# Weight preparation of a decoder layer in six steps: casts placed behind the sums and the evictions, sample rows transposed later

## The chip, the core and the metric

The kernel runs on one core of one Trainium2 chip. The metric is the device time of one execution in microseconds (us). The engines are named as in the profile: PE is TensorE (matmul; PEld its weight loads), DVE is VectorE, ACT is ScalarE, POOL is GpSimd, SP is SyncE, which here only issues transfers. Each engine works through its own queue in order.

## The reference, cut to what matters

One layer of a decoder trunk, for a prompt of 1024 tokens and 8 × 4 sample tokens, 1056 columns in all, width 1024, hidden width 2816:

```python
def trunk_layer(x, ...):
    h = layer_norm(ALPHA * x + 0.5 * swiglu(x, f1_w1, f1_w3, f1_w2), ln1_g, ln1_b)
    z = h @ w_in + b_in                      # 42 blocks of 128 columns: q, k, v, gMLP, gates
    ...                                      # dilated attention (3 groups), gMLP branch
    mix = (sigmoid(ga) * (att @ w_oa) + sigmoid(gb) * (yb @ w_ob)) @ w_out
    h = layer_norm(ALPHA * h + mix, ln2_g, ln2_b)
    h = layer_norm(ALPHA * h + 0.5 * swiglu(h, f2_w1, f2_w3, f2_w2), ln3_g, ln3_b)
def swiglu(x, w1, w3, w2):
    return (silu(x @ w1) * (x @ w3)) @ w2
```

The outputs are `h`, the last keys and values of each attention group, and the normalised rows of the open gMLP chunk.

## The kernel before, in words

**Arithmetic.** Everything is fp32. A product is made of three fp32r matmuls: each operand is split into a high half (a cast on ACT, line 253) and a low half (a subtraction on DVE, line 254), and high·high, high·low and low·high are added up in PSUM (`mm3`, line 242). Columns are worked in four chunks of 264.

**Seven products.** Most weight blocks go through a Strassen scheme of the Winograd form: two blocks times two chunk pairs take seven products instead of eight, in the order 1, 2, 6, 7, 5, 4, 3. This is done in `hidden` (the hidden blocks of both feed-forwards), `seven` (their down-projections) and `pair` (13 pairs of blocks of the input projection, `f` = 0 to 12). After each product its PSUM banks are evicted, partly on ACT (in `pair` line 1034), partly on DVE (line 1043), and `between` runs. There are three `mm` banks and five `ax` banks.

**Weight preparation.** `prep` makes the weights of the next block in the time of the present one. It is a Python generator: each `next` traces one step. It loads the raw weights `ab` (line 376) and `cd` (line 377) into a pool of two buffers, forms the sums `s12` (lines 386 and 387) and `s34` (392 and 394) on POOL, or on DVE where the block has 768 columns instead of 1024 (the down-projections) and for the first blocks, and splits `ab`, `s12`, the last part of `cd` (called `dd`) and `s34` into high and low halves. Products 1 and 2 use `ab`, 6 and 5 use `s12`, 7 and 3 use `s34`, 4 uses `dd`. The first step is traced when the present block begins, the next ones by `between` after its products 1, 2, 6 and 7.

**Order.** A planner orders the instructions of each engine: it goes by the order of tracing and by priorities, and by when it estimates an instruction to be ready. Loads and evictions have raised priority (`high_priority`, `urgent`). `fenced` adds an ordering: what is traced inside it comes, on DVE, ACT and SP (not on POOL), behind the last eviction traced so far. The background queues (`tick`, `step`) are fenced; the steps of `prep` are not.

**Sample rows.** In the pair stage, after each of the nine pairs that hold queries, keys and values, `sample_rows` transposes the 32 sample columns of the two blocks on PE (line 1375), copies them out on DVE (1377) and stores them from SP (1381, 1386). It is a background generator that is resumed three times after each product and pauses first.

Of the kernel before, what the change touches and what calls it, by code (L numbers as in the profile page):

```python
# [16 lines left out]
ALU = mybir.AluOpType  # L17
# [4 lines left out]
P = 128  # L22
D = 1024
# [36 lines left out]
REST = 3  # L60
GAP = 4
AFTER = 100
LATE = 16
MID = 3
HOP = (4, 1, 4)
# [18 lines left out]
class Trunk:  # L84
# [285 lines left out]
    def prep(self, src, f, H, engine):  # L370

        nc = self.nc
        lo, hi, n = slice(0, H), slice(H, 2 * H), 2 * H
        with self.tc.high_priority(offset=URGENT):
            ab, cd = self.R([P, D])[:, :n], self.R([P, D])[:, :n]
            nc.sync.dma_start(ab, src[1])
            dma = nc.sync.dma_start(cd, src[0])
        self.copy_state(dma, 2)
        tt = engine.tensor_tensor
        ah, al = self.W([P, D]), self.W([P, D])  # L380
        self.split(ah[:, :n], al[:, :n], ab)
        if f == LASTW2:
            h34, l34 = self.held([P, D], F32R), self.held([P, D], F32R)
        yield
        s12 = self.Q([P, D])
        tt(s12[:, lo], cd[:, lo], cd[:, hi], op=ALU.add)  # L386
        tt(s12[:, hi], s12[:, lo], ab[:, lo], op=ALU.subtract)  # L387
        yield
        s34 = self.Q([P, D])
        h12, l12 = self.W([P, D]), self.W([P, D])  # L390
        self.split(h12[:, :n], l12[:, :n], s12[:, :n])
        tt(s34[:, lo], ab[:, lo], cd[:, lo], op=ALU.subtract)  # L392
        yield
        tt(s34[:, hi], ab[:, hi], s12[:, hi], op=ALU.subtract)  # L394
        part = lambda h, l, o=0: [((h, l), o + k * P) for k in range(H // P)]
        if n == D:
            dd = self.S([P, D], F32R)
            self.split(dd[:, lo], dd[:, hi], cd[:, hi])
            p4 = part(dd[:, lo], dd[:, hi])
        else:  # L400
            p4 = []
            for h, l, w in ((ah, al, D - n), (h12, l12, H - (D - n))):
                o = H + len(p4) * P
                self.split(h[:, n : n + w], l[:, n : n + w], cd[:, o : o + w])
                p4 += part(h, l, n)[: w // P]
        yield
        if f != LASTW2:
            h34, l34 = self.S([P, D], F32R), self.S([P, D], F32R)
        self.split(h34[:, :n], l34[:, :n], s34[:, :n])
        self.L[f] = {  # L410
            1: part(ah, al), 2: part(ah, al, H), 5: part(h12, l12), 6: part(h12, l12, H),
            7: part(h34, l34), 3: part(h34, l34, H), 4: p4,
        }
        yield

    def product(self, t, p, f, first):
        while any(p not in t for t in self.T):
# [257 lines left out]
    def ffn(self, w13, w2p, w2, i, mode, resid):  # L675
        nc, preps = self.nc, {}
        plain = PLAIN[: 1 if i == 0 else 2]
        blocks = [f for f in range(FB) if f not in plain] + [FB + g for g in range(NG * (KB // 2))]
        after = dict(zip(blocks, blocks[1:]))

        def begin(f):
            if f < FB:
                preps[f] = self.prep(w13[f], f, KH * P, nc.gpsimd if f > 2 else nc.vector)
            else:
                preps[f] = self.prep(w2p[f - FB], f, HP, nc.vector)
            next(preps[f])

        if i == 0:
            self.lns = {}
            self.T, self.L = ({}, {}), {}  # L690
            units = self.lead_in(w13)
            self.new_x(1)
            self.consts()
            s0, s1 = (self.spread(j, self.Y, self.A, self.nc.vector) for j in range(2))
            begin(1)
            with self.tc.high_priority(offset=URGENT):
                for k in range(2):
                    self.load_x(self.nc.sync, 3, k, 0, KH)
            for c, work in enumerate((((2,), s0, s0, 1), ((3,), s0, 1, 1), (s1, s1, s1, 1), (1, s0))):
                self.hidden8(units, 0, c)  # L700
                for x in work:
                    if isinstance(x, tuple):
                        self.new_x(*x)
                    else:
                        next(preps[x] if x == 1 else x, None)
            self.bg.extend((s0, s1))
        else:
            lead, s1 = self.early
            lns, self.lns = self.lns, {}
            self.drain(lns[NC - 2])  # L710
            self.step(self.bg, 1)
            begin(1)
            for c in range(NC):
                self.drain(lns.pop(c))
                if c == NC - 1:
                    self.bg.append(s1)
                    self.step(self.bg, 2)
                for f, u in zip(plain, lead):
                    self.hidden8(u, f, c)
                    if c:  # L720
                        with self.chained():
                            next(preps[1], None)
            lead = self.early = None
        self.sqs = {}
        self.Y = self.A = None
        loads = deque(self.load_sums(resid))
        total = len(loads)

        def ready(f):
            for _ in preps.pop(f):  # L730
                pass
            if f in after:
                begin(after[f])

        def between(f, bg, slow=0):
            if after.get(f) in preps:
                next(preps[after[f]], None)
            self.tick(bg, slow)

        def load(n):  # L740

            with self.tc.high_priority(offset=URGENT):
                while loads and total - len(loads) < n:
                    loads.popleft()()

        for f in blocks[: FB - len(plain)]:
            ready(f)
            if f == FB - 1:
                load(2)
            count = iter(range(1, 8))  # L750

            def step():
                between(f, STEPS["strassen"])
                if f == FB - 1:
                    load(min(HEAD, 2 + 4 * next(count)))

            self.hidden(f, step)
            del self.L[f]
        self.T = ({}, {})
        self.normed = [None] * NC  # L760
        self.out(w2, i, mode, ready, between, load)

    def load_hidden(self, f):
# [61 lines left out]
    def out(self, w2, i, mode, ready, between, load):  # L825
# [101 lines left out]
        for c in range(NC):  # L927
            early = 6 if c == 0 else 0
            if mode != "out":
                self.hold_normed(c)  # L930
                if c == 2:
                    self.early = [self.unit(self.a["wzp"][n], slot=True, ahead=AFTER) for n in range(CHUNKED)]
            for n in range(KB):
# [14 lines left out]
    def tables(self):  # L948
# [8 lines left out]
        for g in range(3):  # L957
            nc.sync.dma_start(oh[g], a["ohP"][:, g])
        yield from self.pause(LATE)
        for g in range(3):  # L960
# [16 lines left out]
        nc.sync.dma_start(rs, a["relS"])  # L977
        yield from self.pause(LATE)
        for i, pair in enumerate(PAIRS):
# [107 lines left out]
    def widen(self):  # L1087
# [13 lines left out]
        preps = {}  # L1101
# [15 lines left out]
        for n in range(CHUNKED, NLEAD):  # L1117
            w = self.unit(a["wzp"][n])
            if n == NLEAD - 1:
                begin(0)  # L1120
            for c in (1, 3, 0, 2):
                self.gate8(w, DENSE[n], c, AF.Sigmoid, STEPS["lead"], 1)
                if n == NLEAD - 1:
                    next(preps[0], None)
        self.A = None
        for f in range(NZ):
            for _ in preps.pop(f):
                pass
            if f < NZ - 1:
                begin(f + 1)  # L1130

            def between():
                if f + 1 in preps:
                    next(preps[f + 1], None)
                self.tick(STEPS["strassen"], 1)

            self.pair(f, between)
            del self.L[f]
# [230 lines left out]

    def sample_rows(self, *blocks):  # L1370
        nc, a = self.nc, self.a
        yield from self.pause(4)
        p = self.ax_tile()[:NS, : 2 * P].rearrange("p (s x) -> p s x", s=2)
        for x, (_, t) in enumerate(blocks):
            nc.tensor.transpose(p[:, x], t[:, NP:], self.ident)
        st = self.M([NS, 2, P])
        nc.vector.tensor_copy(st, p)
        for x, (nb, _) in enumerate(blocks):
            s, g, hp = nb // 6, (nb % 6) // 2, nb % 2
            L = GROUPS[g][0]  # L1380
            nc.sync.dma_start(
                self.sD[g, s, 2 * hp : 2 * hp + 2].rearrange("h t e -> t h e"),
                st[:, x].rearrange("t (h e) -> t h e", h=2),
            )
            if s:
                nc.sync.dma_start(a[f"ws{g}"][:, L - 4 :, 256 * (s - 1) + P * hp : 256 * (s - 1) + P * hp + P], st[:, x])
# [522 lines left out]
```

## Time and profile before

| | |
|---|---|
| time, median of 3 runs | 2154.41 us (2153.32 to 2157.72) |
| time of the profiled execution | 2154.51 us |
| its span | 2152.5 us |
| PE busy | 2122.6 us, 99% |
| DVE, ACT, POOL busy | 1549.5, 889.4, 317.1 us |

The span runs from the first to the last instruction of the program; the time of the execution lies 2.0 us above it. By stretch: from 50 to 475 us the hidden blocks of the first feed-forward run, to 670 its down-projection, from about 790 to 1060 the pairs of the input projection, to 1490 attention, gMLP and output projections, to 1920 and 2085 the second feed-forward. A line of the timeline gives start, duration, engine, line, operation, tiles (output<-inputs) and count; brackets give the idle time of the engine before it and what ended it. W, S, R, Q and M are the tile pools: W and S hold split weights, R raw weights, Q sums.

### The profile page before, as it was taken

To read this page: it belongs to the slowest core of one execution; us is meant where nothing else is said; L and a number is where in the kernel's file an instruction comes from. 1 tells how busy PE (TensorE), PEld (TensorE's weight loads), DVE (VectorE), ACT (ScalarE), POOL (GpSimd) and SP (SyncE) were. 2 spreads that over 40 slices of the span, in tenths; PEclk is the share of its full clock that TensorE was granted. 3 is DMA by queue.
4 is the path that set the end of the run, shared out by engine and by line. 5 is a ranking of instruction groups with operands and counts; after the bars stand their busy time and mean duration, and the time that the engine had idled before them with its cause. 6 is when DMAs were issued, how large, how long until landed. Compare 5 with 4: busy or idle time off the path is not lost.

```text
span 2152.5 us, 43254 instructions
## 1 busy us (share of the span) xinstructions
PE 2122.6 (99%) x17307; PEld 2085.6 (97%) x17307; DVE 1549.5 (72%) x2727; ACT 889.4 (41%) x1680; POOL 317.1 (15%) x249
## 2 busy tenths in 40 slices
PE   9999999999999999999999999999999999999997
PEld 8999999999999999999988889999999999999997
DVE  8877767747789834777767758787667777657887
ACT  5444444422124634333476544164444444421224
POOL 0432322200000011323000000000323323100000
PEclk9999999999999999999999999999999999999998
DMA  4444555598885335676865765423454554596852
GB/s 155 145 140 170 183 166 168 189 338 315 327 325 176 130 103 177 201 231 198 296 211 187 223 190 177 154 110 110 144 174 156 183 173 153 194 408 267 311 186 81
DMA packets 168377, 426.51 MB, mean 198 GB/s; under 512 B 24352, under 2 KB 59792, under 8 KB 165488
## 3 DMA queue, kind: packets, MB, share of 16 engines
q1 hardware_dynamic: 167744, 423.21, 56.4%
q8 instruction: 135, 2.21, 0.4%
q10 hardware_dynamic: 432, 0.54, 0.1%
q14 instruction: 66, 0.54, 0.1%
HBM read 304.31 MB, written 165.57 MB: 218 GB/s over the span
## 4 chain that ended last, share of the span: by engine, by line
PE 89%; DVE 4%; DMA 4%; POOL 1%; issue 1%; ACT 0%; SPq 0%; ACTq 0%; DVEq 0%; POOLq 0%
PE ax L242 46%; PE mm L242 39%; DMA R<-wz 1%; PE ax L1206 1%; DMA M<-kv 1%; DMA S<-cD 1%; PE ax L1255 1%; PE ax L1232 1%; DVE W L254 1%; DMA S<-hD 0%; DVE S L632 0%; POOL Q L392 0%; POOL Q L387 0%; DVE S L254 0%; PE ax L621 0%
## 5 line engine op out<-in xcount | busy, mean ns | idle before, releaser
L242 PE MATMUL mm<-S,W 128*128 128x264 f32 x5400 | 713.6, 287 | 8.0 <-ACT S L253 2.3
L242 PE MATMUL ax<-S,W 128*128 128x264 f32 x5400 | 708.6, 285 | 1.3 <-ACT S L1034 1.1
L242 PEld LDWEIGHTS mm<-S,W 128*128 128x128 f32 x5400 | 677.1, 189 | 21.0 <-issue 7.0
L242 PEld LDWEIGHTS ax<-S,W 128*128 128x128 f32 x5400 | 678.5, 189 | 4.0 <-ACT S L1034 2.4
L242 PE MATMUL ax<-S,S 128*128 128x264 f32 x3240 | 475.9, 284 | 1.0 <-ACT S L1034 0.5
L242 PEld LDWEIGHTS ax<-S,S 128*128 128x128 f32 x3240 | 427.7, 188 | 1.7 <-DVE S L1043 0.9
L242 PE MATMUL mm<-S,S 128*128 128x264 f32 x2280 | 359.4, 286 | 2.6 <-DVE S L925 2.6
L242 PEld LDWEIGHTS mm<-S,S 128*128 128x128 f32 x2280 | 311.0, 189 | 3.9 <-issue 2.9
L253 ACT CAST W<-R 128x256 fp32r<-128x256 f32 (+2 forms) x175 | 130.6, 764 | 307.5 <-PE mm L242 139.9
L386 POOL TENSOR_TENSOR Q<-R 128x512 f32<-128x512 f32 x49 | 68.1, 1390 | 800.8 <-DMA R<-w13a 198.2
L254 DVE TENSOR_TENSOR W<-R,W 128x256 fp32r<-128x256 f32 (+2 forms) x175 | 154.6, 887 | 23.3 <-ACT W L253 21.7
L253 ACT CAST W<-Q 128x1024 fp32r<-128x1024 f32 (+1 forms) x78 | 76.8, 984 | 217.2 <-POOL Q L387 88.1
L820 DVE SCALAR_TENSOR_TENSOR S<-ax,S 128x264 f32<-128x264 f32 x240 | 99.7, 429 | 66.1 <-PE ax L242 65.7
L462 DVE TENSOR_TENSOR S<-ax,M 128x264 f32<-128x264 f32 x82 | 32.6, 433 | 144.7 <-PE ax L242 144.7
L254 DVE TENSOR_TENSOR S<-Q,S 128x1024 fp32r<-128x1024 f32 (+1 forms) x78 | 113.6, 1456 | 5.5 <-ACT S L253 5.4
L110 POOL CAST S<-ones 128x1 fp32r<-128x1 f32 x36 | 12.5, 355 | 675.7 <-PE ax L242 226.0
L254 DVE TENSOR_TENSOR W<-Q,W 128x1024 fp32r<-128x1024 f32 (+1 forms) x78 | 90.6, 1161 | 29.6 <-ACT W L253 29.6
L253 ACT CAST S<-Q 128x1024 fp32r<-128x1024 f32 (+1 forms) x78 | 76.7, 984 | 68.4 <-PE ax L242 49.8
L254 DVE TENSOR_TENSOR S<-S,M 128x528 fp32r<-128x528 f32 x72 | 84.6, 1175 | 2.5 <-ACT M L253 0.7
L253 ACT CAST S<-R 128x512 fp32r<-128x512 f32 (+1 forms) x62 | 42.0, 677 | 98.9 <-DMA sumsA<-S 40.6
L387 POOL TENSOR_TENSOR Q<-Q,R 128x512 f32<-128x512 f32 x49 | 81.0, 1653 | 2.7
L394 POOL TENSOR_TENSOR Q<-R,Q 128x512 f32<-128x512 f32 x49 | 79.7, 1627 | 1.2
(209 smaller groups left out, 2042.5 us busy)
## 6 DMA issues: line engine op xcount, KB each, us to landing
ws<-st SPq DMA_DIRECT2D x144, 256.0 KB
S<-sumsA SPq DMA_DIRECT2D x63, 528.0 KB
S<-sumsB SPq DMA_DIRECT2D x63, 528.0 KB
M<-kv SPq DMA_DIRECT2D x96, 256.0 KB
sumsA<-M SPq DMA_DIRECT2D x90, 264.0 KB
sumsB<-M SPq DMA_DIRECT2D x90, 264.0 KB
R<-w13b SPq DMA_DIRECT2D x44, 512.0 KB
R<-w13a SPq DMA_DIRECT2D x42, 512.0 KB
```

Source lines behind the costliest of these rows:

```text
L110: self.nc.gpsimd.tensor_copy(t[:, 0, :1] if len(shape) == 3 else t[:, :1], self.ones[:, :1])
L242: mm = lambda a, b, s, e: nc.tensor.matmul(o, a[:, cc], b, start=s, stop=e, skip_group_check=True)
L253: a = self.nc.scalar.copy(hi, src)
L254: b = self.nc.vector.tensor_tensor(lo, src, hi.bitcast(F32), op=ALU.subtract)
L386: tt(s12[:, lo], cd[:, lo], cd[:, hi], op=ALU.add)
L387: tt(s12[:, hi], s12[:, lo], ab[:, lo], op=ALU.subtract)
L394: tt(s34[:, hi], ab[:, hi], s12[:, hi], op=ALU.subtract)
L462: go(one, 5, False, lambda x: tt(h[:, x, 1], one[x], p7[:, x], op=ALU.add))
L820: nc.vector.scalar_tensor_tensor(y(x, r, e), bank[x], HALF, y(x, r, e), op0=ALU.mult, op1=ALU.add)
L1206: m = nc.tensor.matmul(pS[h][:, r, :nk], q[e, i * P : (i + 1) * P], k[e, k0 : k0 + nk], start=True, stop=True)
L1232: nc.tensor.transpose(pT[r][:, h, o], s[:, r, h, o], self.ident)
L1255: nc.tensor.matmul(pv[0][e, (i % 4) * P : (i % 4 + 1) * P], V[:, i - (nb - 1) + b, e], sT[:, r, h, b * P : b * P + P], start=b == 0, stop= ...
```

## The change

Four things change. In `prep` the split of `ab` moves from the first step to the second, behind the sums of `s12`; the split of `s12` moves from the third step to the fourth, and the third step holds only the first sum of `s34`. All steps but the first are traced inside `fenced`, through a new function `advance`, in both the feed-forwards and the pairs. The preparation of the very first pair is resumed once more before its pair begins. `sample_rows` pauses for 8 resumptions instead of 4.

```diff
+ROWS = 8
...
             dma = nc.sync.dma_start(cd, src[0])
         self.copy_state(dma, 2)
         tt = engine.tensor_tensor
-        ah, al = self.W([P, D]), self.W([P, D])
-        self.split(ah[:, :n], al[:, :n], ab)
         if f == LASTW2:
             h34, l34 = self.held([P, D], F32R), self.held([P, D], F32R)
         yield
         s12 = self.Q([P, D])
         tt(s12[:, lo], cd[:, lo], cd[:, hi], op=ALU.add)
         tt(s12[:, hi], s12[:, lo], ab[:, lo], op=ALU.subtract)
+        ah, al = self.W([P, D]), self.W([P, D])
+        self.split(ah[:, :n], al[:, :n], ab)
         yield
         s34 = self.Q([P, D])
+        tt(s34[:, lo], ab[:, lo], cd[:, lo], op=ALU.subtract)
+        yield
         h12, l12 = self.W([P, D]), self.W([P, D])
         self.split(h12[:, :n], l12[:, :n], s12[:, :n])
-        tt(s34[:, lo], ab[:, lo], cd[:, lo], op=ALU.subtract)
-        yield
         tt(s34[:, hi], ab[:, hi], s12[:, hi], op=ALU.subtract)
...
+    def advance(self, gen):
+        if gen is not None:
+            with self.fenced():
+                next(gen, None)
...
         def between(f, bg, slow=0):
-            if after.get(f) in preps:
-                next(preps[after[f]], None)
+            self.advance(preps.get(after.get(f)))
             self.tick(bg, slow)
...
                 if n == NLEAD - 1:
-                    next(preps[0], None)
+                    for _ in range(2 if c == 2 else 1):
+                        next(preps[0], None)
...
             def between():
-                if f + 1 in preps:
-                    next(preps[f + 1], None)
+                self.advance(preps.get(f + 1))
                 self.tick(STEPS["strassen"], 1)
...
     def sample_rows(self, *blocks):
         nc, a = self.nc, self.a
-        yield from self.pause(4)
+        yield from self.pause(ROWS)
```

## The prediction

> **What bounds the kernel now.** I read the page first, then the busy times by stretch, then the waits, then the timeline where TensorE (PE) stood idle.
>
> ```profile
> span 2152.5 us, 43254 instructions
> PE 2122.6 (99%) x17307; PEld 2085.6 (97%) x17307; DVE 1549.5 (72%) x2727; ACT 889.4 (41%) x1680; POOL 317.1 (15%) x249
> ...
> 50.00:475.00 425.00, 425.00 (x3490) 425.00 (x3490) 301.19 (x416) 177.72 (x314) 119.87 (x76) 1.00 0.54 181
> 475.00:670.00 195.00, 192.84 (x1537) 188.40 (x1536) 150.39 (x318) 44.09 (x71) 3.82 (x14) 0.99 0.85 318
> 790.00:1060.00 270.00, 266.17 (x2159) 263.53 (x2158) 184.04 (x312) 108.23 (x208) 63.08 (x44) 0.99 0.62 207
> 1060.00:1300.00 240.00, 235.39 (x1973) 211.45 (x1972) 160.82 (x478) 139.12 (x370) 4.13 (x11) 1.00 0.65 210
> 1490.00:1920.00 430.00, 430.00 (x3538) 430.00 (x3537) 296.07 (x418) 176.11 (x311) 111.22 (x72) 1.00 0.54 186
> 1920.00:2085.00 165.00, 164.91 (x1353) 164.69 (x1352) 130.90 (x275) 38.78 (x61) 0.84 (x2) 1.00 0.78 292
> 2085.00:2152.00 67.00, 54.90 (x439) 54.10 (x437) 50.66 (x110) 28.66 (x63) 0.00 (x0) 0.92 0.17 65
> ```
>
> PE is busy for 2122.6 of 2152.5 us, so an edit that removes no matmul can win at most what PE stands idle, 29.9 us, and what a lowered clock costs. The stretches (start:end, length, then busy time of PE, weight load, DVE, ACT, POOL, then granted clock, DMA share, GB/s) place it. The change edits weight preparation, which runs in the Strassen blocks of the two feed-forwards (50 to 475 and 1490 to 1920), their down-projections (475 to 670 and 1920 to 2085) and the input-projection pairs (790 to 1060). In both Strassen stretches PE is busy in every microsecond (425.00 of 425.00, 430.00 of 430.00): nothing can be won there. The second down-projection has 0.09 us to give. The idle 12.1 us of the end and 4.6 us of the attention stretch belong to other code. What this change can reach is the pair stretch: 270.00 − 266.17 = 3.83 us idle, and a clock of 0.99.
>
> The waits of that stretch, then its worst place in time (start, duration, engine, line; in brackets the idle time before and what ended it):
>
> ```profile
> ACT W L253 <- POOL Q L387: 79.2, 11, 13.2
> ...
> PE ax L1375 <- ACT S L1034: 1.7, 2, 1.2
> PE ax L242 <- ACT S L1034: 0.5, 2, 0.2
> PE ax L242 <- DVE S L1043: 0.4, 1, 0.4
> ...
> 931.08 2.46 POOL L392 TENSOR_TENSOR Q<-R,R 128x512 f32<-128x512 f32 x1
> 933.46 3.07 PE L242 MATMUL mm<-S,W 128*128 128x264 f32 x24
> 933.49 1.74 POOL L387 TENSOR_TENSOR Q<-Q,R 128x512 f32<-128x512 f32 x1
> 935.26 1.05 ACT L253 CAST W<-Q 128x1024 fp32r<-128x1024 f32 x1 [13.15 <-POOL Q L387]
> 936.22 1.47 ACT L1034 ACTIVATE S<-ax,qb 128x256 f32<-128x256 f32 x5
> 937.75 0.40 PE L1375 MATMUL ax<-ident,S 128*32 128x128 f32 x2 [1.21 <-ACT S L1034]
> 938.38 4.98 PE L242 MATMUL ax<-S,W 128*128 128x264 f32 x24 [0.23 <-ACT S L1034]
> ```
>
> ACT's queue is in order. The cast of `s12` (line 253, W<-Q) stands in it ahead of the evictions of line 1034, and waits for the GpSimd sum of line 387, which ends at 935.23. ACT does nothing for 13.15 us; the eviction of the pair just finished starts at 936.22 only, the transposes of the sample rows (line 1375), which read that pair's tile, hold PE for 1.21 us, and the next product waits 0.23 more for its bank. Then its 24 matmuls take 4.98 us. The same kind of wait stands 11 times in the stage, 79.2 us in all; most of it PE never feels. How often PE felt it, the pair periods tell, from one second product (24 matmuls mm<-S,W) to the next:
>
> ```profile
> 889.39 3.11 PE L242 MATMUL mm<-S,W 128*128 128x264 f32 x24
> 910.36 3.07 PE L242 MATMUL mm<-S,W 128*128 128x264 f32 x24
> ...
> 957.74 1.50 PE L242 MATMUL mm<-S,W 128*128 128x264 f32 x11
> 978.35 1.88 PE L242 MATMUL mm<-S,W 128*128 128x264 f32 x14
> 998.99 3.11 PE L242 MATMUL mm<-S,W 128*128 128x264 f32 x24
> 1020.26 2.00 PE L242 MATMUL mm<-S,W 128*128 128x264 f32 x15
> 1040.68 1.52 PE L242 MATMUL mm<-S,W 128*128 128x264 f32 x11
> ...
> 911.75 1.05 ACT L253 CAST W<-Q 128x1024 fp32r<-128x1024 f32 x1 [4.89 <-POOL Q L387]
> 914.59 3.44 PE L242 MATMUL ax<-S,W 128*128 128x264 f32 x24 [0.23 <-ACT S L1034]
> 1000.46 1.05 ACT L253 CAST W<-Q 128x1024 fp32r<-128x1024 f32 x1 [5.55 <-POOL Q L387]
> 1002.68 3.20 PE L242 MATMUL ax<-S,W 128*128 128x264 f32 x24 [0.58 <-ACT S L1034]
> ```
>
> (Rows of a window that cuts a group show fewer of the 24; the starts stand.) The periods are 20.97, 23.10 (to 933.46), 24.28, 20.61, 20.64, 21.27 and 20.42 us. An undisturbed one with two transposes takes 20.63 (mean of 20.61 and 20.64), one without, as the last two, 20.42. So the losses are 0.34, 2.47, 3.65, 0, 0, 0.85.
>
> One of them has another cause:
>
> ```profile
> 924.27 0.68 DVE L254 TENSOR_TENSOR S<-R,S 128x512 fp32r<-128x512 f32 x1
> 925.00 1.22 DVE L254 TENSOR_TENSOR S<-Q,S 128x1024 fp32r<-128x1024 f32 x1
> 926.87 0.68 DVE L1043 SCALAR_TENSOR_TENSOR S<-ax,S 128x256 f32<-128x256 f32 x2
> 927.61 2.63 PE L242 MATMUL ax<-S,S 128*128 128x264 f32 x16 [0.38 <-DVE S L1043]
> ```
>
> Here two low-half subtractions of the preparation run on DVE ahead of the eviction that frees the bank. PE's matmuls start 0.12 us apart (3.07 us for 24, less the pipelined tail); by start distances this place costs about 1.05 us of the 2.47. The other 1.42 lie at 913 to 915, behind the cast at 911.75.
>
> **The change, part by part.**
>
> *The cast of `s12` moves from the third step to the fourth* (behind the third product's evictions) and every step but the first is issued, through `advance`, behind the last evictions traced on ACT, DVE and SP. No instruction is added or removed: still four casts and four subtractions a block. Before, this cast stood at 935.26 while the next block's second product (933.46) ran; in the new order it comes after that block's third product, whose 24 matmuls are those of the row at 938.38: at 20.42 / 7 = 2.9 us for each of a pair's seven products, some 5 us later than 935. The sums keep their place, since POOL is not among the fenced engines, so the sum that was ready at 935.23 is ready before the cast comes up. The three stalls behind it go: 1.42 + 3.65 + 0.85 = 5.92 us. What is late next: the product that needs `h12` is the third of the block after, one period of 20.6 us on; a cast (1.05) and a subtraction of 1.22 (the row at 925.00 is of that shape) leave some 15 us. Nothing waits.
>
> *The `dd` split now stands behind the `s12` split in the same step.* The buffer of `cd` comes free one cast and one subtraction later, at most 1.05 + 1.22 = 2.3 us; SP's load of the next `cd` waits for it, and behind that load in SP's queue stand the state copies and the sample keys and values. The sums that use it start up to 2.3 us later, but their reader now comes 5 us later. I take 0. If it is not hidden, it is one late key slab a pair; DVE's waits for those are bounded below.
>
> *The split of `ab` moves from the first step to the second*, behind the two sums of `s12` in trace order. In the Strassen and pair stages the sums are on POOL, it has most of a block before its first use, and costs 0. In the down-projections the sums run on DVE:
>
> ```profile
> 602.97 0.95 DVE L254 TENSOR_TENSOR W<-R,W 128x768 fp32r<-128x768 f32 x1
> 603.84 0.55 DVE L386 TENSOR_TENSOR Q<-R 128x384 f32<-128x384 f32 x1
> 603.98 1.97 PE L242 MATMUL ax<-S,W 128*128 128x264 f32 x14 [0.25 <-DVE W L254]
> ```
>
> Here the low half of `ab` is made at the moment of its use, and PE waits 0.25 us for it. With both sums (2 × 0.55) ahead of it, it is ready 1.1 us later. Twelve blocks in each of two down-projections: from 0 (the loads land early, and the queue is ordered by when things are ready) to 24 × 1.1 = 26.4 us. The rest of both stretches has 192.84 and 164.91 us of PE time in 195 and 165, so hardly a block is late now; I take the low end, half a block's worth, +0.5 us.
>
> *The sample rows pause 8 instead of 4.* At three resumptions per product the two transposes come after the third product of the next pair instead of the second. Two transposes, one copy on DVE and two to four transfers on SP for each of 9 pairs go about 2.9 us later; their reader is the sample attention of the following group of pairs. PE's work is the same. The stall in front of them (1.7 us in two waits) is inside the 5.92 already. With both edits the pair's last eviction is over long before; 0 more.
>
> *The extra resume of the first pair's preparation* meets a generator that, by the diff, still stops five times: it does nothing, 0.
>
> Sum: −5.92 + 0.5 = −5.4 us against the profiled execution's 2154.51 us (span 2152.5 and 2.0 around it; the median of the three is 2154.41, so it is a typical one): 2149.1 us.
>
> The lost clock is part of this. After the 1.21 us stall PE ran 24 matmuls in 4.98 us where the same group took 3.44 at 914.59, so 1.5 us of the 3.65 are clock, not waiting. I count it, since the sum is made against this execution; that it is no fixed part of the stall is rival (d).
>
> **The rivals.**
> (a) *DVE takes ACT's place.* The subtraction of `s12` leaves the quiet start of the block and comes, with `dd`'s, between the third and fourth products' evictions, just where the stall at 927.61 arose. If PE then waits in three to five of the thirteen pairs as it did there, 3 to 5 × 1.05 = 3.2 to 5.3 us come back: 2152.3 to 2154.4, no change to tell. For it: DVE is busy 184 of 270 us in this stretch and stops for key slabs. Against: the fence puts these subtractions behind the evictions already traced.
> (b) *The stall is hidden anyway, or the planner finds another order with it.* If the 11 waits of 79.2 us remain in another form and PE feels as much: 2154.5. Against it: the cast cannot be issued before the third product's eviction.
> (c) *Slower: the late `ab` split starves PE in the down-projections.* Price 1.1 us at each block whose loads land late; where a wait passes 1.2 us, the lost clock adds 1.5 (as at 938.38), 2.6 in all. To lose 4.3 us net of the 5.92, four blocks at 2.6 or ten at 1.1 must be hit; six late blocks at 2.6 give 2154.5 − 5.9 + 15.6 = 2164.2. For it: the wait at 603.98, in a stretch whose DMA share is 0.85. Against: PE idles 2.2 us there in all, mostly elsewhere.
>
> (d) *The clock loss was this execution's own.* Behind 0.58 us idle the row at 1002.68 shows 3.20 us for 24 matmuls, no lowered clock, and there is one such event in the stage. If the runs mostly lack it, the change wins 5.4 − 1.5 = 3.9 us: 2150.6. Against it: the waits of 1.21 and 0.23 us lie within 1 us of each other, and one row of this kernel shows the loss behind them. The Trainium skill ("TensorE: Matmul & The Clock Gate", section "Why this matters for your kernels") lets the clock fall only behind idle gaps above about 3 us, which speaks for (d); the trace differs from it (4.98 us behind 1.21 us idle), so the measurement decides.
>
> **How the numbers follow.** The three runs before lie within 0.2% (2153.32 to 2157.72), so 0.2%, 4.3 us, is about what a measurement tells from no change; the limit of faster is 2150.1. The forecast 2149.1 (own range 2146.5 to 2150.5, the low end where the 1.05 and 0.34 us go too and the 0.5 does not come): 0.50. Rival (a): 0.18. Rival (b): 0.12. Rival (c): 0.12, of which a third is a small loss inside 0.2%. Rival (d): 0.08. The forecast's own range ends above the limit of 2150.1, so 0.03 of its 0.50 counts as same: faster 0.47, same 0.03 + 0.18 + 0.12 + 0.04 + 0.08 = 0.45, slower 0.08. The range 2146.0 to 2156.5 reaches over (a), (b) and (d) and leaves out the tails of (c) and what lies below the low end.
>
> **What would show it.** Right: in the pair stretch ACT's wait for line 387 falls from 79 us to near nothing, the cast W<-Q comes about 9 us into a pair instead of just before its start, the periods are all 20.6 or 20.4, the granted clock is 1.00 there, and PE no longer waits before line 1375, which runs one product later. The Strassen stretches stay at full PE. (a) shows as PE waits on DVE line 1043; (c) as PE waits on DVE W of line 254 between 475 and 670 or 1920 and 2085. I am wrong if the pair stretch is clean and the time is the same: then another stage, above all attention, where the order of everything may shift, gave it back.

## The result and the profile after

| | before | after |
|---|---|---|
| median of 16 runs each | 2156.26 us (2150.10 to 2159.71) | 2161.23 us (2157.73 to 2163.88) |
| profiled execution, its span | 2154.51, 2152.5 us | 2160.51, 2157.9 us |

The ratio after to before is 1.0024, with a 95% interval of 1.0017 to 1.0031: the change made the kernel slower by about 5 us, where a gain of 5.4 us was forecast. Of the profiled difference of 6.0 us, 5.4 lie in the span.

The page of the kernel after, and its busy times by stretch (start:end, length, then PE, weight load, DVE, ACT, POOL, granted clock, DMA share, GB/s). Line numbers shift by one to five: 242 is now 243 (matmul), 253 and 254 are 254 and 255 (split), 386 and 387 are 385 and 386 (sums of `s12`), 376 and 377 are 377 and 378 (loads), 1034, 1043 and 1375 are 1039, 1048 and 1380.

```profile
span 2157.9 us, 42869 instructions
PE 2122.3 (98%) x17307; PEld 2086.3 (97%) x17307; DVE 1527.6 (71%) x2727; ACT 881.7 (41%) x1680; POOL 285.9 (13%) x249
...
50.00:475.00 425.00, 425.00 (x3486) 425.00 (x3485) 284.56 (x417) 172.84 (x311) 103.86 (x76) 1.00 0.54 182
790.00:1060.00 270.00, 270.00 (x2224) 269.77 (x2223) 197.44 (x329) 111.86 (x215) 63.42 (x44) 1.00 0.66 217
1490.00:1920.00 430.00, 428.85 (x3519) 428.22 (x3519) 281.64 (x417) 172.02 (x310) 95.59 (x72) 1.00 0.54 185
1920.00:2085.00 165.00, 160.18 (x1294) 159.97 (x1293) 126.25 (x266) 37.10 (x59) 0.37 (x2) 0.98 0.79 291
```

The pair stretch (790 to 1060) is clean: PE busy 270.00 of 270.00 at clock 1.00. The second down-projection (1920 to 2085), which was full before (164.91 of 165), is idle for 4.82 us at clock 0.98. That is where most of the time went. Fixed windows drift against the work when something ahead gets shorter, so I cut both traces at the same work, the starts of a second product (in us from the start of the span):

| from, to | before | after | difference |
|---|---|---|---|
| start, first down-projection (466.02; 464.72) | 466.0 | 464.7 | −1.3 |
| to the first pair (806.74; 808.30) | 340.7 | 343.6 | +2.9 |
| to the end of the pairs (1058.99; 1053.31) | 252.3 | 245.0 | −7.2 |
| to the second feed-forward (1494.39; 1490.32) | 435.4 | 437.0 | +1.6 |
| to block 22 there (1902.24; 1898.51) | 407.9 | 408.2 | +0.3 |
| to the end (2152.5; 2157.9) | 250.3 | 259.4 | +9.1 |

The pairs won 7.2 us, the end of the second feed-forward lost 9.1, two other places 4.5.

**The pairs.** The longest wait of ACT between 780 and 1060, and rows of the timeline at the place that the prediction showed as its worst:

```profile
ACT S L1039 <- PE ax L243: 113.9, 33, 7.1
```

```profile
930.34 1.74 POOL L386 TENSOR_TENSOR Q<-Q,R 128x512 f32<-128x512 f32 x1
932.23 3.07 PE L243 MATMUL mm<-S,W 128*128 128x264 f32 x24
937.94 0.85 ACT L1039 ACTIVATE S<-ax,qb 128x264 f32<-128x264 f32 x2 [3.55 <-PE ax L243]
938.04 0.38 PE L1380 MATMUL ax<-ident,S 128*32 128x128 f32 x2
938.69 1.04 ACT L254 CAST W<-Q 128x1024 fp32r<-128x1024 f32 x1
```

ACT's long waits are now for PE's products, as an eviction should wait; the wait for the GpSimd sum (79.2 us before) is gone. The sum ends at 932.08; its cast stands behind an eviction and runs at 938.69, 6.5 us after the second product's start. The transposes run at 938.04 with no idle time in front of them.

**The second down-projection.** First before, then after, rows picked from the timelines: SP's loads of raw weights (R<-w2pb), what SP issues ahead of them, and what DVE, ACT and PE do with them.

```profile
1902.72 0.33 SPq L376 DMA_DIRECT2D R<-w2pb  x1
1911.83 0.33 SPq L377 DMA_DIRECT2D R<-w2pb  x1
1922.79 0.84 ACT L253 CAST W<-R 128x768 fp32r<-128x768 f32 x1 [8.65 <-PE ax L242]
```

```profile
1902.21 10.01 SPq L783 DMA_DIRECT2D S<-sumsB  x9
1910.46 0.28 DVE L255 TENSOR_TENSOR W<-R,W 128x128 fp32r<-128x128 f32 x1
1912.00 2.69 PE L243 MATMUL ax<-S,W 128*128 128x264 f32 x20 [0.66 <-DVE W L255]
1913.19 1.58 SPq L788 DMA_DIRECT2D S<-hD  x2
1917.13 1.63 SPq L788 DMA_DIRECT2D S<-hD  x2
1921.00 2.91 SPq L853 DMA_DIRECT2D M<-hidB  x3
1925.50 0.33 SPq L377 DMA_DIRECT2D R<-w2pb  x1
1933.04 1.49 ACT L254 CAST W<-R 128x768 fp32r<-128x768 f32 x3 [2.41 <-DMA R<-w2pb]
1933.92 1.25 PE L243 MATMUL ax<-S,W 128*128 128x264 f32 x4 [4.82 <-ACT W L254]
1935.85 3.28 PE L243 MATMUL ax<-S,W 128*128 128x264 f32 x14
```

Before, block 24's `ab` is loaded at 1902.72, and at 1922.79 its cast waits for PE, not for data: early enough. After, the load goes out at 1925.50; ACT waits for its landing, PE waits 4.82 us for the cast, and then runs at about half clock: 14 matmuls in 3.28 us where the same group takes 1.97 (stretch 604, below). Yet the last read of the raw buffers was over at 1910.74 (1910.46 and 0.28). The load goes out 14.8 us after that. SP had begun nine loads of sums at 1902.21, while the buffers were still in use, and issues the last of them by 1912.22; then it issues ten more transfers (among them four loads of hD and three of hidden rows), and only then the weights. The DMA engines are full meanwhile: from 1895 to 1930 their busy share is 0.99 to 1.07 in every 5 us of the kernel after, at 395 to 426 GB/s (1.02 to 1.04 before, at 402 to 415), so what stands ahead of a load takes its time.

Of the 9.1 us of the last row of the table, the 4.82 us wait, two smaller ones (0.38 us at 1909.97 and 0.66 at 1912.00) and 5.3 us at clock 0.50, which cost 2.65, make 8.5.

### The profile page after: what moved, and what is told of

It reads as the page before. It is cut to its first block, busy times and chain, and to the rows that moved or that the text cites. A ratio compares the mean times of both kernels' runs of the same rounds, so it can differ in the third digit from the quotient of the medians.

```text
span 2157.9 us, 42869 instructions
## 1 busy us (share of the span) xinstructions
PE 2122.3 (98%) x17307; PEld 2086.3 (97%) x17307; DVE 1527.6 (71%) x2727; ACT 881.7 (41%) x1680; POOL 285.9 (13%) x249
## 4 chain that ended last, share of the span: by engine, by line
PE 89%; DVE 5%; DMA 4%; issue 1%; ACT 1%; SPq 0%; ACTq 0%; DVEq 0%; POOL 0%
PE ax L243 48%; PE mm L243 36%; PE ax L1211 1%; DMA S<-cD 1%; DMA R<-w2pb 1%; PE ax L1260 1%; PE ax L1237 1%; DVE W L255 1%; DMA S<-xc 1%; DVE S L638 1%; DVE S L1590 0%; DVE S L255 0%; PE mm L1556 0%; DVE S L561 0%; PE ax L627 0%
## 5 line engine op out<-in xcount | busy, mean ns | idle before, releaser
L255 DVE TENSOR_TENSOR S<-Q,S 128x1024 fp32r<-128x1024 f32 (+1 forms) x78 | 89.0, 1142 | 46.2 <-ACT S L254 46.1
L472 ACT ACTIVATE S<-S 128x528 f32<-128x528 f32 x82 | 48.5, 638 | 165.1 <-DVE S L471 165.1
L473 DVE TENSOR_TENSOR S<-S,M 128x264 f32<-128x264 f32 x82 | 93.5, 1168 | 14.8 <-ACT S L472 13.9
L464 ACT COPY M<-ax 128x264 f32<-128x264 f32 x82 | 28.9, 381 | 140.8 <-issue 93.1
L466 ACT COPY M<-ax 128x264 f32<-128x264 f32 x82 | 30.7, 380 | 135.4 <-PE ax L243 135.3
L386 POOL TENSOR_TENSOR Q<-Q,R 128x512 f32<-128x512 f32 x49 | 71.9, 1467 | 0.1
```

Of the source, the lines that this page charges most:

```text
L255: b = self.nc.vector.tensor_tensor(lo, src, hi.bitcast(F32), op=ALU.subtract)
L464: go(one, 1, True, lambda x: copy(r1[:, x], one[x]))
L466: go(one, 6, False, lambda x: copy(u2[:, x], one[x]))
L472: lambda x: nc.scalar.activation(h[:, x], h[:, x], AF.Silu),
L473: lambda x: tt(h[:, x, 0], h[:, x, 0], r1[:, x], op=ALU.mult),
```

## The experiments

In the table, "delay" is the issue of block 24's `ab` load, counted from the start of block 22's second product; "end" is the time from that mark to the end of the span.

| kernel | fence in feed-forward | delay | PE's loss there | end | ratio to before |
|---|---|---|---|---|---|
| before | – | 0.5 | 0 | 250.3 | 1 |
| e1 | none | 0.9 | 0 | 250.1 | 0.9972 |
| e10 | all but last five hidden blocks | 18.7 | 0.9 | 251.2 | 0.9977 |
| e6 | down-projections only | 19.2 | 1.4 | 251.8 | 0.9978 |
| e2 | all, old steps | 23.1 | 3.1 | 255.5 | 1.0002 |
| after | all | 27.0 | 5.1 | 259.4 | 1.0024 |
| e5 | hidden blocks only | 26.9 | 5.4 | 260.4 | 1.0024 |
| e11 | last five hidden blocks only | 27.0 | 5.1 | 260.2 | 1.0025 |

(PE's loss is the step between two matmul starts less the usual one; what the clock takes comes on top.)

**Is it the fence in the feed-forwards?** e1 takes it out there and leaves the rest:

```diff
         def between(f, bg, slow=0):
-            self.advance(preps.get(after.get(f)))
+            if after.get(f) in preps:
+                next(preps[after[f]], None)
```

> The changed kernel with one thing undone: in the feed-forwards the steps of the preparation are resumed without the fence, as before; the new order of the steps stays everywhere, and the pairs keep the fence. Theory run-ahead (the fence holds the preparation of the next block behind the evictions of the present one, so weight loads are issued up to a block later, and at the start of the second down-projection they stand behind a flood of other loads): block 24's weights are split by about 1924 again, the 4.8 us wait of PE near 1929 is gone, the pair stretch stays clean; 2161 - 9 = about 2152, faster than before by some 4 us. Theory split order (the split of ab behind two sums on DVE makes weights late): the wait stays, about 2161.

Measured: 2149.04 us, ratio 0.9972 (0.9963 to 0.9981). Its stretches of the pairs and of 1880 to 2085, and block 24's load and cast:

```profile
790.00:1060.00 270.00, 270.00 (x2223) 269.77 (x2222) 198.18 (x332) 112.22 (x216) 63.33 (x44) 1.00 0.67 218
1880.00:2085.00 205.00, 204.91 (x1681) 204.63 (x1681) 151.32 (x319) 46.08 (x74) 1.02 (x2) 1.00 0.80 304
```

```profile
1897.97 0.33 SPq L377 DMA_DIRECT2D R<-w2pb  x1
1900.61 4.33 SPq L784 DMA_DIRECT2D S<-sumsB  x4
1917.60 0.84 ACT L254 CAST W<-R 128x768 fp32r<-128x768 f32 x1 [8.04 <-PE ax L243]
```

The load is back ahead of the sums, the cast waits for PE again, both stretches are full. So the fence in the feed-forwards costs the whole loss. e1 keeps the later split of `ab`: without the fence that step starves nothing.

**The fence without the new steps.** e2 is the kernel before with every step but the first traced inside `fenced`, in the old order and with the old pause.

```diff
-            if after.get(f) in preps:
-                next(preps[after[f]], None)
+            self.advance(preps.get(after.get(f)))
 ...
-                if f + 1 in preps:
-                    next(preps[f + 1], None)
+                self.advance(preps.get(f + 1))
```

> The kernel before with the fence alone: every step but the first is traced behind the last evictions, in feed-forwards and pairs; the order of the steps and the pause of 4 are the old ones. Theory run-ahead: weight loads of blocks 22 to 24 as late as in the changed kernel (block 24's about 1925), PE waits there for several us, about 2158 to 2162. Theory split order: no wait there, since ab is split in the first step; 2150 to 2156. In the pair stretch the cast of s12 comes one product earlier than in the changed kernel (about 6 us into a pair): clean if the sum is there by then.

Measured: 2155.17 us, ratio 1.0002 (0.9992 to 1.0012). (The trace is of an execution of 2151.39 us. Six of its twelve runs lie between 2151.4 and 2153.7 us, six between 2156.6 and 2161.2; the trace stands for the first six only.) Its pairs, its second down-projection, and a stall of PE in the pairs:

```profile
790.00:1060.00 270.00, 268.45 (x2207) 267.68 (x2206) 192.05 (x331) 110.38 (x213) 62.60 (x44) 1.00 0.65 218
1880.00:2085.00 205.00, 201.19 (x1641) 200.28 (x1640) 150.73 (x318) 46.83 (x76) 0.37 (x2) 1.00 0.80 303
```

```profile
985.45 1.22 DVE L254 TENSOR_TENSOR S<-Q,S 128x1024 fp32r<-128x1024 f32 x1
987.07 1.11 PE L242 MATMUL ax<-S,S 128*128 128x264 f32 x7 [1.55 <-DVE S L1047]
```

The fence alone clears most of the pairs and alone brings a late load, smaller than with the new steps (delay 23.1 against 27.0, and no lowered clock in this trace). The wait is what the first expectation named, the time lies in the range of the second: neither holds alone. What is left in the pairs is rival (a)'s mechanism: a low-half subtraction on DVE ahead of an eviction.

**The change in the pairs alone.** e3 keeps the old `prep`, unfenced, for the feed-forwards and gives the pairs the new steps, the fence and the pause of 8. Its edit is against the kernel after; the bodies of the two functions are left out here.

```diff
+    def prep_late(self, src, f, H, engine):   # the new steps; prep itself keeps the old ones
 ...
         def between(f, bg, slow=0):
-            self.advance(preps.get(after.get(f)))
+            if after.get(f) in preps:
+                next(preps[after[f]], None)
 ...
         def begin(f):                          # in the pairs
-            preps[f] = self.prep(a["wz7"][f], f, KH * P, nc.gpsimd if f else nc.vector)
+            preps[f] = self.prep_late(a["wz7"][f], f, KH * P, nc.gpsimd if f else nc.vector)
```

> New steps, fence and pause of 8 in the pairs alone; the feed-forwards prepare as before. Theory run-ahead and theory split order both: the first 790 us and the second down-projection are as before, the pair stretch gains 7 us; about 2156 - 7 = 2149. If the order of everything behind the pairs shifts by chance of the planner, it lands elsewhere, 2146 to 2158, with no late weights of line 254 in either down-projection.

Measured: 2149.13 us, ratio 0.9973 (0.9964 to 0.9982), as e1: in the feed-forwards, old steps or new make no difference once there is no fence.

**The sample rows' pause alone.** e4 is the kernel before with a pause of 8.

```diff
-        yield from self.pause(4)
+        yield from self.pause(8)
```

> The kernel before with the pause of 8 alone. Theory (the stall comes from the cast in ACT's queue, the transposes only show it): the bank of the next product waits for the same eviction, so the pair stretch still loses some 4 to 6 of its 7 us, 2154 to 2157. Rival (the transposes are what holds PE): the pair stretch is nearly clean, 2150 or less.

Measured: 2156.94 us, ratio 1.0010 (1.0002 to 1.0019). PE's waits between 780 and 1060:

```profile
PE ax L242 <- ACT S L1034: 3.1, 5, 1.4
PE ax L242 <- DVE S L1043: 1.5, 2, 0.9
```

The wait in front of the transposes is gone, and the next product waits for its bank instead: the transposes were not the cause, only the first to feel the late eviction. From the other side, e8, which is e1 with a pause of 4:

```diff
-ROWS = 8
+ROWS = 4
```

> The fence in the pairs alone, new steps, and the old pause of 4 before the transposes. Theory (the cast was the cause, the transposes only showed it): the pair stretch is as clean as with the pause of 8, 270.00 us of 270 or 0.5 us less, about 2149 to 2150. Rival (both are needed): several us of waits before the transposes come back, 2152 to 2155.

Measured: 2149.28 us, ratio 0.9972 (0.9963 to 0.9981), and its pair stretch is full too (270.00 of 270.00 busy). With clean pairs the longer pause is not needed; in the kernel before it wins nothing.

**Is it the fence or the order of the steps that clears the pairs?** e9 is the kernel after with the fence off everywhere; e12 is the kernel before with the fence in the pairs only, in the old steps.

```diff
         def between(f, bg, slow=0):      # e9, feed-forwards
-            self.advance(preps.get(after.get(f)))
+            if after.get(f) in preps:
+                next(preps[after[f]], None)
 ...
             def between():               # e9, pairs
-                self.advance(preps.get(f + 1))
+                if f + 1 in preps:
+                    next(preps[f + 1], None)
 ...
                 if f + 1 in preps:       # e12, against the kernel before
-                    next(preps[f + 1], None)
+                    with self.fenced():
+                        next(preps[f + 1], None)
```

> The changed kernel with the fence off everywhere: new order of the steps and pause of 8 alone. Theory (only the fence keeps the cast of s12 behind the evictions; without it the planner hoists it to the moment at which the sum should be ready): the cast waits for GpSimd ahead of evictions again, ACT waits over 50 us for the sums in the pair stretch, which loses 5 to 7 us; no late weights in the down-projection; 2154 to 2157. Rival (the later step suffices): clean pair stretch and about 2149.

> The kernel before with the fence in the pairs alone: old steps, old pause. Theory (the fence is what cleans the pairs): the pair stretch gains at least 5 of its 7 us, 2149 to 2151. Rival (the new step order is needed as well): DVE's evictions are held by subtractions as in one pair of the run with the fence and the old steps, several of them, 2153 to 2156.

Measured: e9 2158.04 us, ratio 1.0012 (1.0003 to 1.0020); e12 2151.12 us, ratio 0.9980 (0.9970 to 0.9990). The longest wait of ACT and a wait of PE in the pairs of e9, then the one place of e12 where PE waits:

```profile
ACT W L254 <- POOL Q L386: 85.2, 11, 11.9
...
PE ax L243 <- ACT S L1040: 4.6, 6, 1.5
```

```profile
987.99 1.22 DVE L254 TENSOR_TENSOR S<-Q,S 128x1024 fp32r<-128x1024 f32 x1
989.13 0.77 DVE L1043 SCALAR_TENSOR_TENSOR S<-ax,S 128x264 f32<-128x264 f32 x2
989.61 2.79 PE L242 MATMUL ax<-S,S 128*128 128x264 f32 x11 [2.69 <-DVE S L1043]
```

Without the fence ACT's casts wait for the GpSimd sums again, 11 times and 85.2 us, though their step is traced one product later: what rival (b) describes comes about where the fence is missing, and the forecast's reason "behind the third product's evictions" holds only through the fence. With the fence the old steps already win most; one stall on DVE stays, and a pair of 25.0 us instead of 20.7. The new steps remove that one.

**Where in the feed-forward does the fence cost?** Four kernels are the change with the fence in a part of the feed-forwards (always in the pairs). `f` counts a feed-forward's blocks; from `FB` on they are the down-projection's.

```diff
-            self.advance(preps.get(after.get(f)))
+            g = preps.get(after.get(f))
+            if f < FB:              # e5;  e6: f >= FB
+                self.advance(g)     # e10: f < FB - 5 or f >= FB;  e11: FB - 5 <= f < FB
+            elif g is not None:
+                next(g, None)
```

> The changed kernel with the fence off in the two down-projections (the preparation of blocks 23 to 33), on in their hidden blocks (2 to 22) and in the pairs. Theory run-ahead, that the lag is built up in the hidden blocks: blocks 22 and 23 are prepared as late as in the changed kernel, block 24's load is issued near 1925 and PE waits 3 us or more near 1929; about 2158 to 2161. If the lag arises in the down-projection itself: as with no fence in the feed-forwards, about 2150.

> The opposite: the fence off in the hidden blocks, on in the down-projections and the pairs. If the lag is built up in the hidden blocks: blocks 22 and 23 are loaded as before (about 1845 and 1865), at most a small wait at block 24, whose load now stands later in SP's queue; 2149 to 2153. If it arises in the down-projection: a wait of 3 us or more near 1925, 2156 to 2160.

> The changed kernel with the fence off in the last five hidden blocks of each feed-forward (17 to 21) and on elsewhere. If the price is paid at the one boundary, where the down-projection's loads flood SP's queue, and the lag is no more than the buffers hold (it does not add up over twenty blocks): blocks 22 and 23 are loaded early again and the time is 2149 to 2152, like the fence off in all hidden blocks. If the lag adds up over the blocks: 2155 or more.

> The opposite: of all feed-forward blocks only the last five hidden ones are fenced, and the pairs. If the price is paid at the boundary: the whole loss is there, block 24's load near 1925, a wait of 4 us or more near 1929, 2158 to 2161.

Measured: e5 2160.87 us, 1.0024 (1.0015 to 1.0033); e6 2150.61 us, 0.9978 (0.9970 to 0.9987); e10 2148.96 us, 0.9977 (0.9968 to 0.9985); e11 2159.67 us, 1.0025 (1.0017 to 1.0034). Block 24's load in e6, e10 and e11, in this order, and the stretch 1880 to 2085 of each:

```profile
1917.61 0.33 SPq L377 DMA_DIRECT2D R<-w2pb  x1
```

```profile
1880.00:2085.00 205.00, 203.73 (x1669) 203.31 (x1668) 149.58 (x317) 46.24 (x74) 0.37 (x2) 1.00 0.81 307
```

```profile
1915.76 0.33 SPq L377 DMA_DIRECT2D R<-w2pb  x1
```

```profile
1880.00:2085.00 205.00, 204.24 (x1673) 203.81 (x1672) 150.03 (x318) 46.35 (x74) 0.37 (x2) 1.00 0.81 305
```

```profile
1925.20 0.33 SPq L377 DMA_DIRECT2D R<-w2pb  x1
```

```profile
1880.00:2085.00 205.00, 198.99 (x1609) 198.14 (x1607) 148.05 (x311) 45.70 (x77) 0.76 (x2) 0.98 0.84 315
```

The fence in the last five hidden blocks alone (e11) costs as much as the whole change, and leaving it out there alone (e10) gives the gain back. The fence in the down-projection itself delays the same load too, but by 19 us instead of 27, and PE feels 0.9 to 1.4 us of that. From 18.7 to 27.0 us of delay the loss grows from 0.9 to 5.1 us, about half a microsecond for each microsecond of delay. By that line, an estimate, some 17 us are covered; no run lies between 0.9 and 18.7.

**One more raw buffer.** If the load waited only for a free buffer, a third would end it. e7 is the change with three R buffers and 36 slots for S.

```diff
-NSLOT = 37
+NSLOT = 36
 ...
     def R(self, shape, dt=F32):
         self.n += 1
-        return self.rp.tile(shape, dt, tag="R", name=f"R{self.n}")
+        return self.rp.tile(shape, dt, tag="R", name=f"R{self.n}", bufs=3)
```

> The changed kernel with the fence everywhere and three buffers for raw weights instead of two (and 36 slots S instead of 37 to make room). Theory (the fence delays the reads that free the two raw buffers, and so puts the next load behind the flood in SP's queue): with a third buffer the loads of block 24 are issued 15 us or more earlier, the 4.8 us wait goes, and the time is 2150 to 2154. If instead it is the splits themselves that come too late behind the evictions, the loads are early and PE waits all the same, 2157 to 2161. One slot S less may cost by itself in the attention stretch; that would show there.

Measured: 2163.1 us, ratio 1.0027 (1.0015 to 1.0038), outside both expected ranges. The trace is of an execution of 2156.12 us, 7 us under the median; the six others lie between 2159.65 and 2164.29, so it shows how block 24 is prepared, not the whole loss.

```profile
1918.74 0.45 SPq L378 DMA_DIRECT2D R<-w2pb  x1
1918.94 0.96 DVE L255 TENSOR_TENSOR W<-R,W 128x768 fp32r<-128x768 f32 x1 [2.54 <-ACT W L254]
1928.11 0.61 ACT L254 CAST W<-R 128x256 fp32r<-128x256 f32 x2 [9.20 <-DMA R<-w2pb]
1931.80 0.43 DVE L825 SCALAR_TENSOR_TENSOR S<-mm,S 128x264 f32<-128x264 f32 x1
1932.15 0.55 DVE L385 TENSOR_TENSOR Q<-R 128x384 f32<-128x384 f32 x1
1934.01 0.83 ACT L254 CAST W<-Q 128x768 fp32r<-128x768 f32 x1 [5.29 <-DVE Q L386]
1934.89 1.25 PE L243 MATMUL ax<-S,W 128*128 128x264 f32 x4 [3.59 <-ACT W L254]
```

The miss teaches something. `ab` is now loaded early (1895.9) and split by 1919.9, but `cd` still goes out at 1918.74; the sums and the cast of `s12` behind them become the late ones, and PE waits 3.59 us for that cast. A block needs both halves: with one buffer more, only one half comes early. But `cd` has landed by 1928.11, where ACT casts a part of it, and the first sum, which reads nothing else, starts 4.0 us later, behind an eviction on DVE. So the steps held behind the evictions are late here too, which is the expectation's other case; this is read from DVE's order. What the late `cd`, the held sums and the fewer S slots cost each was not separated.

## Why the prediction was wrong, point by point

- **Cast of `s12`, −5.92 us:** right in mechanism. The three stalls went, and the two smaller losses that the prediction left standing (1.05 and 0.34 us) went too: −7.2 by the marks. The pairs' signs came: the cast at 938.69 is 8.9 us behind the main group of the pair's first product (929.78), where about 9 were forecast. Two things said of it were loose. The order of the steps does little of it (e9: nothing without the fence), the fence nearly all (e12). And before, the cast at 935.26 did not stand just before its pair's start but 4.2 us behind that group (931.04).
- **`dd` split, 0; sample rows, 0; extra resume, 0:** no cost showed in the pairs, PE never waits there; e8, with the old pause, does as well. The extra resume and the `dd` split were not tried alone.
- **Split of `ab` in the down-projections, +0.5 us:** the place was right, the mechanism wrong. Waits on line 255 did come, two of them in the first down-projection:

```profile
494.85 1.97 PE L243 MATMUL ax<-S,W 128*128 128x264 f32 x14 [0.42 <-DVE W L255]
604.09 1.97 PE L243 MATMUL ax<-S,W 128*128 128x264 f32 x14 [0.98 <-DVE W L255]
```

  That is 1.4 us in all, where the prediction had a row of 0.25 us. But in both places the split still runs ahead of the sums (at 493.84 and 603.08, the first sums at 494.71 and 603.95), and e1 and e9, which keep the late split and drop the fence, lose nothing there that the kernel before does not. So a split behind two sums is not what is late. With the fence and the old steps (e2) these waits are 0.4 us; how the new steps add to them is not shown.
- **The step that failed** is the cost of the fence in the feed-forwards, which the sum puts at nothing without a reason. The prediction has the steps go "behind the last evictions traced on ACT, DVE and SP" and costs that only in the pairs; of the Strassen stretches it says that nothing can be won there, since PE is busy in every microsecond, and it looks for no loss. PE is still so after (425.00 of 425.00, and 390.00 of 390.00 from 1490 to 1880). What the fence took there was not PE's time but the lead of the preparation. Before, the last read of block 23's raw buffers was over at 1896.35 (its subtraction at 1896.07, of the same shape as that at 1910.46); after, at 1910.74. These 14.4 us (18.1 counted from the start of block 22's second product) let nine loads of sums pass in front of block 24's load, which then goes 22.8 us later (26.5 from that start). The prediction followed this chain once, from a split to a buffer to a load in SP's queue, for `cd` (at most 2.3 us, taken as 0); for the fenced steps of the feed-forwards it did not.
- **Rival (c)** named the stage and the sign, at a chance of 0.12. Its price, 1.1 or 2.6 us a late block and six blocks, was wrong in kind: it was mainly one block, at 4.82 us and a lowered clock.
- **Rival (d)** is not settled: e1 wins 6.7 us between medians (2155.7 to 2149.04), though it has the new wait in attention too; without the clock all losses of the pairs together make 5.92 + 1.05 + 0.34 − 1.5 = 5.8 us. But the interval of e1's ratio (0.9963 to 0.9981) makes 4.1 to 8.0 us and holds both. In e4 and e9, whose pairs stall as well, the clock of the pair stretch is 1.00.
- **The time is given back also in attention**, as the last sentence feared, but by 1.6 us only. A transpose there waits for a load:

```profile
PE ax L1514 <- DMA S<-zD: 2.1, 1, 2.1
```

  Most kernels with clean pairs have this wait too (e1, e3, e8, e10 and e11 1.7 to 2.6 us, e5 0.8, e6 1.3; e7 two of 0.3), and before has not; with stalls left in the pairs it is 2.2 us in e12, at most 0.7 in e4 and e9, and none in e2. A reason may be that the pairs end some 6 us earlier and the load of sample rows does not come as much earlier. This is read from the traces, not tried. Of the first down-projection's +2.9 us, 1.1 are the growth of the waits on line 255 (1.4 against 0.3); with no fence in the feed-forward (e1) the stretch is 340.7 again, the rest is not taken apart.

Two things stay open. That the load is late because it stands behind the sums' loads and the other transfers in SP's queue, with the DMA engines full, is read from the order of issue; an experiment that moves it ahead of them was not run. And why the new steps make the fence dearer (delay 27.0 against 23.1 in e2) was not separated.

## What to carry to other kernels

An ordering that costs no busy time on any engine can still cost lead: for each instruction it holds back, ask which buffer it frees, which load waits for that buffer, and what stands in front of that load in its queue at the next change of stage. A stage that is full in every microsecond is no proof that an edit is free there; the bill may come where the next stage begins. Put an ordering only where the wait is: with the fence in the pairs and none in the feed-forwards (e1, e3, e8) the change gives 0.9972 or 0.9973 instead of 1.0024.

## What the runs showed of the hardware

The lowered clock does not follow from the length of a wait alone. Behind the 1.21 us wait of before it fell (0.68 over 937.70 to 943.00); behind e12's 2.69 us it fell (0.54 over 989.60 to 993.00), and behind after's 4.82 us (0.50 over 1933.90 to 1939.20); behind e2's 2.82 us at the same block it did not (nor in e4 and e9, whose waits in the pairs reach 1.4 and 1.5 us):

```profile
1926.84 0.76 PE L242 MATMUL ax<-S,W 128*128 128x264 f32 x4 [2.82 <-ACT W L253]
1927.93 1.88 PE L242 MATMUL ax<-S,W 128*128 128x264 f32 x14
```

Here 14 matmuls take 1.88 us, against 3.28 in the kernel after. The Trainium skill ("TensorE: Matmul & The Clock Gate", section "Why this matters for your kernels") asks for no idle gaps of TensorE above about 3 us. The trace agrees at 4.82 and 2.82 us and differs at 1.21 and 2.69. So in this kernel a wait of 1 to 3 us is a risk of about 1.5 us (4.98 against 3.44 us for 24 matmuls; 3.4 us at 0.54), not a sure price.
